# Layer norm statistics of a diffusion layer: from diagonals and full products to turned lines picked by one-pass products

## The chip, the core and the metric

The kernel runs on one core of one Trainium2 chip. The metric is the device time of one execution in microseconds; the figure for a kernel is the median of its runs. A core has TensorE (PE in the profile; its weight loads are PEld), VectorE (DVE), ScalarE (ACT), GpSimd (POOL) and SyncE (SP, here the queue of most transfers). They run side by side, each through its own list of instructions in order, and wait for each other by semaphores.

## The reference, cut to what matters

One layer over 1024 latent tokens of 1024 channels: modulation, two attention branches, a merge, a residual with layer norm, a convolutional feed-forward block, and a second residual with layer norm. The change is in the two layer norms alone:

```python
def _layer_norm(x, g, b):
    xf = x.astype(jnp.float32)
    mu = jnp.mean(xf, axis=-1, keepdims=True)
    var = jnp.mean(jnp.square(xf - mu), axis=-1, keepdims=True)
    return ((xf - mu) * lax.rsqrt(var + LN_EPS) * g + b).astype(x.dtype)
...
        x = _layer_norm(DEEPNORM_ALPHA * x + gate1 * y, ln1_g[l], ln1_b[l])

        h = x * (1.0 + scale2) + shift2
        y = _conv_ffn(h, w_up[l], conv_w[l], conv_b[l], w_down[l])
        x = _layer_norm(DEEPNORM_ALPHA * x + gate2 * y, ln2_g[l], ln2_b[l])
```

## The kernel before, in words

**Layout.** Activations lie with channels on the 128 partitions and tokens along the free dimension: eight channel tiles (KT = 8) of 128 x 1024. A mean over channels is therefore a sum over partitions and over eight tiles, and a statistic of a token has to reach all 128 partitions before it can be applied.

**Products.** A full-precision product is three one-pass products (`mm3`, L375 to L378): each operand is split by `split` (L366 to L373) into a high part (float32r) and a low part (the float32 rest, also float32r), and high x high, high x low and low x high are summed. A product of two plain float32 operands is issued as one instruction and shows as two records.

**The layer norm in pieces.** The first norm (after the product with w_out, tile y) is done in three pieces of tokens: a0 (512 tokens), a1 (256) and a2 (256). The second norm (after the down product) is done in b0 (512) and b1 (256) by the same function, `ln_steps` (L1498); its last 256 tokens go another way (`finish`, L2086), with the tokens on the partitions, and are not touched. While the channel tiles are produced, `ln_add` (L1469) sums each tile into zs and its squares into zq (ScalarE squares, VectorE or GpSimd adds, L1478 and L1479). With n = 4 or 2 tiles of 128 tokens in a piece, `ln_steps` then returns a list of steps:

- stats: 2n small products with a column of ones (L1511, L1512) give n sums and n sums of squares per token, in the PSUM tile st (128 tokens on the partitions). VectorE makes mean, square and variance (L1513, L1515, L1516), GpSimd raises to the power -1/2 (L1518), VectorE multiplies mean by it (L1519). The result is rs and mr, n columns each, tokens on partitions.
- diags: VectorE multiplies the identity by each column (L1458), which gives a diagonal of 128 x 128 per token tile, dgr for rs and dgm for mr.
- cast: two float32 products of a 128 x 128 matrix of ones with the diagonals (L1528) put each statistic on all 128 partitions (bcr, bcm in PSUM); ScalarE copies them out (L1530).
- eight applications, one per channel tile: multiply by the first (VectorE, L1535), subtract the second (VectorE or GpSimd, L1537), then the piece's outputs (for the first norm ScalarE's affine maps, L1558, and the low part, L1564).

**What sets the order.** TensorE's instructions run in the order in which the code issues them (L1390, a manual schedule for TensorE to the end). The steps of a norm are put between the products of the next work by a clock of issued columns: `tick` (L1484) adds the width of a group of three products divided by 0.8, so 640 for 512 columns and 320 for 256, and issues the next step of the list once its gap is reached, keeping what is left over. The gaps are constants, in the order first, diags, cast, first application, each further one:

```python
LN1_F = 4500.0, 5100.0, 100.0
LN1_D = (2500.0, 2000.0, 2000.0, 2500.0), (300.0, 3700.0, 300.0, 500.0), (100.0, 1000.0, 300.0, 500.0)
LN2_D = 4000.0, 2800.0, 2000.0, 1200.0, 1300.0
LN2_E = 3500.0, 1500.0, 1500.0, 500.0, 400.0
```

a0's steps fall among the y products of the second half (`y_pair`, L1650). a1's sums come at the end of the last y products, its other steps among the first products of the up projection (tile u, `up_mm`, L1759). a2's first three steps are put between a1's applications (L1677 to L1684): sums after a1's second application, diags after its fourth, cast after its eighth. b0's fall among the down products (tile p, `product`, L1951), b1's among the products of the last 256 tokens (tile yt, from L2104). VectorE, ScalarE and GpSimd are ordered by the framework's scheduler in this part, and in its order an instruction waits for those ahead of it on its engine.

**Small tiles and neighbours.** In the first norm the small PSUM tiles (st, bcr, bcm) share two banks (`sml`, L1332). The temporaries (`tm`, L1325: zs, zq, squares, diagonals) share four slots. Two weight tiles of the up projection (L1796 to L1798) are issued so that their work on VectorE comes behind a1's last diagonal (`issue_after`).

## Time and profile before

| what | value |
|---|---|
| median of 3 runs | 1521.83 us (1521.33 to 1522.35) |
| profiled execution, its own time | 1522.45 us |
| its span | 1520.6 us |
| instructions | 21967 |
| granted TensorE clock, mean | 0.998 |
| norm pieces a0, a1, a2: sums start | 816.1, 859.1, 866.3 us |
| norm pieces b0, b1: sums start | 1454.5, 1497.3 us |

The profile is of one execution. Times in it count from the start of the span. In an order of time each line gives the start, the duration, the engine, the line of the code, the operation, the tile written and the tiles read, and the shape; "x2" merges two neighbours, and a bracket tells how long the engine had been idle and who released it. Matmuls are pipelined, and the duration of one holds its way through the array: the distance from one start to the next is what it costs, not the duration.

### The profile page before, as it was taken

How to read it: one execution, taken by the hardware profiler on the slowest of the kernel's cores; microseconds unless marked ns; L12 is line 12 of the kernel's file. 1: busy time of each engine (PE TensorE's matmuls, PEld its weight loads, DVE VectorE, ACT ScalarE, POOL GpSimd, SP SyncE). 2: the span in 40 equal slices, each digit the busy share in tenths (PEclk: the TensorE clock that was granted, in tenths of full speed). 3: DMA queues.
4: the chain of work that ended last, by engine and by line, in shares of the span. 5: the costliest groups of instructions: out<-in, count | busy, mean ns of one | idle time of the engine just before them, and what ended most of it. 6: DMA issues, size and time to landing. Idle time of an engine off the chain costs nothing.

```text
span 1520.6 us, 21967 instructions
## 1 busy us (share of the span) xinstructions
PE 1507.5 (99%) x7640; PEld 1267.1 (83%) x7640; DVE 1154.0 (76%) x1735; ACT 800.3 (53%) x1406; POOL 784.7 (52%) x743
## 2 busy tenths in 40 slices
PE   9999999999999999999999999999999999999997
PEld 7888888889988888888888998888888888888886
DVE  7588847629777777787675888988888888657897
ACT  6422223448987777788233564444444444435533
POOL 0375303428896666585533556666677774021053
PEclk9999999999999999999999999999999999999999
DMA  9767673312447654823460322333344446996723
GB/s 376 257 220 256 219 242 110 94 40 66 119 119 170 170 122 105 175 66 105 154 166 22 108 90 101 111 112 111 111 111 111 111 111 192 368 270 207 253 80 111
DMA packets 112161, 229.73 MB, mean 151 GB/s; under 512 B 13521, under 2 KB 27345, under 8 KB 111954
## 3 DMA queue, kind: packets, MB, share of 16 engines
q1 hardware_dynamic: 97040, 199.72, 40.0%
q0 software_dynamic: 10400, 20.19, 8.6%
q10 hardware_dynamic: 4610, 8.42, 1.5%
q8 instruction: 60, 0.98, 0.3%
q14 instruction: 51, 0.42, 0.1%
HBM read 177.09 MB, written 65.87 MB: 160 GB/s over the span
## 4 chain that ended last, share of the span: by engine, by line
PE 44%; DVE 4%; issue 1%; DMA 1%; ACT 1%; POOL 0%; DVEq 0%; SPq 0%; ACTq 0%
PE p L377 3%; PE p L378 3%; PE p L376 3%; PE c L376 2%; PE a L376 2%; PE d L376 2%; PE a L378 2%; PE d L378 2%; PE c L378 2%; PE d L377 2%; PE c L377 2%; PE a L377 2%; PE y L378 2%; PE y L376 2%; PE y L377 2%; PE u L376 1%
## 5 line engine op out<-in xcount | busy, mean ns | idle before, releaser
L1234 DVE TENSOR_TENSOR lo<-pt,hi 128x512 fp32r<-128x512 f32 x188 | 126.8, 686 | 44.4 <-ACT hi L1228 35.0
L373 DVE TENSOR_TENSOR ld<-rd,hd 128x1024 fp32r<-128x1024 f32 x77 | 97.6, 1284 | 49.1 <-ACT hd L368 47.0
L1228 ACT CAST hi<-pt 128x512 fp32r<-128x512 f32 x188 | 108.4, 582 | 41.8 <-PE pt L847 23.5
L368 ACT CAST hd<-rd 128x1024 fp32r<-128x1024 f32 x77 | 79.5, 1050 | 86.5 <-PE p L378 53.0
L856 PE MATMUL av<-hi,VT 128*128 128x512 f32 x236 | 104.3, 443 | 0.2 <-POOL hi L1223 0.2
L377 PE MATMUL p<-ld,hd 128*128 128x512 f32 x264 | 102.8, 389 | 0.5 <-DVE ld L373 0.5
L376 PE MATMUL p<-hd 128*128 128x512 f32 x264 | 103.2, 391 | 0.0
L378 PE MATMUL p<-hd,ld 128*128 128x512 f32 x264 | 102.8, 389 | 0.0
L376 PE MATMUL g<-hh,whg 128*128 128x512 f32 x256 | 99.9, 390 | 0.0
L377 PE MATMUL g<-hl,whg 128*128 128x512 f32 x256 | 99.6, 389 | 0.0
L378 PE MATMUL g<-hh,wlg 128*128 128x512 f32 x256 | 99.6, 389 | 0.0
L856 PE MATMUL av<-lo,VT 128*128 128x512 f32 x236 | 99.3, 422 | 0.1
L373 POOL TENSOR_TENSOR wlg<-wg,whg 128x512 fp32r<-128x512 f32 x32 | 45.1, 1415 | 101.1 <-ACT whg L368 89.4
L793 DVE TENSOR_SCALAR_CACHE_REDUCE p<-s,cvt,nmc 128x1024 f32<-128x1024 f32 x64 | 85.6, 1339 | 11.0 <-PE s L760 7.1
L847 PEld LDWEIGHTS pt<-ident,p 128*128 128x128 f32 x512 | 63.6, 140 | 17.6 <-ACT rb L829 0.4
L802 ACT ACTIVATE p<-p,nm 128x1024 f32<-128x1024 f32 x64 | 73.9, 1155 | 7.0 <-DVE p L793 6.5
L847 PE MATMUL pt<-ident,p 128*128 128x128 f32 x512 | 76.6, 272 | 0.1
L759 PE MATMUL s<-KL,q 128*128 128x512 f32 (+2 forms) x186 | 72.9, 392 | 0.0
L793 DVE TENSOR_SCALAR_CACHE_REDUCE pa<-s,negsink 128x640 f32<-128x640 f32 (+1 forms) x58 | 49.3, 853 | 29.2 <-PE s L760 28.7
L368 ACT CAST wS<-s 128x512 fp32r<-128x512 f32 x76 | 45.3, 621 | 48.5 <-POOL s L1564 47.7
L760 PE MATMUL s<-KL,q 128*128 128x512 f32 (+2 forms) x186 | 69.5, 374 | 0.0
L368 ACT CAST wA<-ru 128x512 fp32r<-128x512 f32 x57 | 35.5, 623 | 63.0 <-PE d L378 34.8
(438 smaller groups left out, 5044.0 us busy)
## 6 DMA issues: line engine op xcount, KB each, us to landing
wml<-in_wmodT_dram SPq DMA_DIRECT2D x48, 512.0 KB
ru<-in_w_up_dram SPq DMA_DIRECT2D x38, 512.0 KB
rd<-td SPq DMA_DIRECT2D x55, 256.0 KB
rd<-sd SPq DMA_DIRECT2D x44, 256.0 KB
rd<-in_w_dn_dram SPq DMA_DIRECT2D x33, 256.0 KB
wm<-in_wmodT_dram SPq DMA_DIRECT2D x16, 512.0 KB
wg<-in_w_g_dram SPq DMA_DIRECT2D x32, 256.0 KB
q<-q SPq DMA_DIRECT2D x64, 128.0 KB
```

The lines of the kernel that those rows point to most:

```text
L368: cast[:] = [nc.scalar.copy(hi, src).ins]
L373: low[:] = [lo_eng.tensor_tensor(out=lo, in0=src, in1=hi.bitcast(F32), op=ALU.subtract).ins]
L376: nc.tensor.matmul(ps, a[0], b[0], start=start, stop=False, skip_group_check=resumed)
L377: nc.tensor.matmul(ps, a[0], b[1], start=False, stop=False, skip_group_check=resumed)
L378: return nc.tensor.matmul(ps, a[1], b[0], start=False, stop=stop, skip_group_check=resumed).ins
L759: nc.tensor.matmul(o, self.q1[:, hs], ks, start=True, stop=False)
L793: nc.vector.tensor_scalar(out=p if self.br else p[:, self.pad + 1:SINK + 1], in0=self.sv[h], scalar1=self.scale()[:, hs] if self.br else - ...
L802: nc.scalar.activation(o, i, AF.Exp, bias=self.nm[:, hs], scale=-1.0, accum_out=acc)
L847: nc.tensor.transpose(tr[:, h * P:(h + 1) * P], src, ident)
L856: nc.tensor.matmul(self.av, v, self.parts[n][low], start=first, stop=self.left == 0)
L1228: nc.scalar.copy(hi, units[u].parts[n])
L1234: e.tensor_tensor(out=lo, in0=src, in1=hi.bitcast(F32), op=ALU.subtract)
```

## The change

The split of the statistics now follows in stats: rs and mr lie side by side in one tile (rm, 2n columns), and VectorE splits them into a high and a low part in a tile sp of 4n columns. A new step, rows, takes the place of diags at the same gap: TensorE transposes sp (operand identr) into the unused right half of the piece's PSUM tile st, which gives 4n lines of 128 tokens, and VectorE copies them to SBUF. In cast, each statistic of each token tile is one product: the stationary operand is a column of a constant, pick, spread over 128 columns; it has ones in the high and the low line of that statistic, so 128 columns of the lines come out, summed, on all partitions. That makes 2n float32r products of 128 columns in place of two float32 products of n x 128. ScalarE's copies stay. The weights that were issued behind a1's last diagonal now come behind a1's row copy. The gaps are unchanged.

```diff
+    pick = {n: ctile([P, 2 * n], R32, f"pick{n}") for n in (2, 4)}
...
-    def diag(cols, n, nm):
-        dg = tm(f"dg{nm}", w=HALF).rearrange("p (a b) -> p a b", b=P)
-        i = nc.vector.tensor_tensor(out=dg[:, 0:n], in0=ident.unsqueeze(1).to_broadcast([P, n, P]),
-                                    in1=cols.unsqueeze(2).to_broadcast([P, n, P]), op=ALU.mult)
-        last_diag[:] = [i.ins]
-        return dg[:, 0:n].rearrange("p a b -> p (a b)")
+    for n in (2, 4):
+        nc.vector.tensor_tensor(out=pick[n], in0=ident[:, 0:2 * n], in1=ident[:, 2 * n:4 * n], op=ALU.add)
...
-            sv.extend(tiny(f"{a}{nm}") for a in ("mv", "m2", "rs", "mr"))
-            mv, m2, rs, mr = sv
+            mv, m2, rm = (tiny(f"{a}{nm}") for a in ("mv", "m2", "rm"))
+            rs, mr = rm[:, 0:n], rm[:, n:2 * n]
...
-        def diags():
-            bcs.extend(diag(c[:, 0:n], n, f"{a}{nm}") for a, c in zip("rm", sv[2:]))
-            diag_ins[nm] = last_diag[0]
+            sp = post.tile([P, 16], R32, tag="sp", name=f"sp{nm}", bufs=2)
+            split(rm[:, 0:2 * n], sp[:, 0:2 * n], sp[:, 2 * n:4 * n], nc.vector, nc.vector)
+            sv.extend((sp, st))
+
+        def rows():
+            sp, st = sv
+            turned = st[0:4 * n, P:2 * P].bitcast(R32)
+            nc.tensor.transpose(turned, sp[:, 0:4 * n], identr)
+            row = tm(f"row{nm}", R32, w=P)[0:4 * n]
+            row_ins[nm] = nc.vector.tensor_copy(row, turned).ins
+            sv[:] = [row]
 
         def cast():
             for i, a in enumerate("rm"):
                 ps = sml(f"bc{a}{nm}")[:, 0:w]
-                nc.tensor.matmul(ps, onesf, bcs[i], start=True, stop=True)
+                for t in range(n):
+                    w1 = pick[n][0:4 * n, i * n + t:i * n + t + 1].to_broadcast([4 * n, P])
+                    nc.tensor.matmul(ps[:, t * P:(t + 1) * P], w1, sv[0], start=True, stop=True)
                 o = post.tile([P, HALF], F32, tag="mrs", name=f"{a}b{nm}", bufs=2)[:, 0:w]
                 nc.scalar.copy(o, ps)
-                bcs[i] = o
+                bcs.append(o)
...
-        return [(first, stats), (gap, diags), (gap1, cast)] + [
+        return [(first, stats), (gap, rows), (gap1, cast)] + [
...
-                with tc.issue_after(diag_ins["a1"]):
+                with tc.issue_after(row_ins["a1"]):
```

More of the change, by code (lines that the diff above doesn't have):

```diff
@@ L1452, in tiny @@
         return post.tile([P, 8], F32, tag="tiny", name=name, bufs=6)
-    last_diag, diag_ins = [], {}
-    def diag(cols, n, nm):
-        dg = tm(f"dg{nm}", w=HALF).rearrange("p (a b) -> p a b", b=P)
-        i = nc.vector.tensor_tensor(out=dg[:, 0:n], in0=ident.unsqueeze(1).to_broadcast([P, n, P]),
-                                    in1=cols.unsqueeze(2).to_broadcast([P, n, P]), op=ALU.mult)
-        last_diag[:] = [i.ins]
-        return dg[:, 0:n].rearrange("p a b -> p (a b)")
+    for n in (2, 4):
+        nc.vector.tensor_tensor(out=pick[n], in0=ident[:, 0:2 * n], in1=ident[:, 2 * n:4 * n], op=ALU.add)
+    row_ins = {}
     sqs = []
```

## The prediction, made before the changed kernel ran

> **What bounds the kernel now.** I read the page first, then TensorE's waits, then the order of time around each of the five norm pieces. The page gives the span and the busy shares:

> ```profile
> span 1520.6 us, 21967 instructions
> PE 1507.5 (99%) x7640; PEld 1267.1 (83%) x7640; DVE 1154.0 (76%) x1735; ACT 800.3 (53%) x1406; POOL 784.7 (52%) x743
> PEclk9999999999999999999999999999999999999999
> ```

> TensorE is busy in 99% of the span, at full granted clock in every slice. The table of waits, TensorE's own, is complete in five lines:

> ```profile
> PE cb L522 <- DVE mhalf L404: 1.1, 1, 1.1
> PE q1acc L378 <- DVE hl L516: 0.5, 1, 0.5
> PE p L377 <- DVE ld L373: 0.5, 1, 0.5
> PE zt L2060 <- DVE zz L1923: 0.3, 1, 0.3
> PE av L856 <- POOL hi L1223: 0.2, 1, 0.2
> ```

> That is 2.6 us of waiting in 1520.6. TensorE's order is written by hand, so whatever is removed from its queue is gained and whatever it waits for is lost, nearly one for one, until about 1511 us; after that only VectorE, ScalarE, GpSimd and the stores run. So the change has two terms: products that get cheaper, and one new instruction per piece, the turning of the split statistics (rows), that TensorE must not start before VectorE is done. Before, the step at that place (diags) was VectorE work alone, and TensorE met the chain only one step later, at cast. The pieces are a0, a1, a2 (first norm, 512, 256, 256 tokens) and b0, b1 (second norm, 512 and 256).

> **The products: removed and added.** The order of time at a0's cast, and at a1's:

> ```profile
> 822.71 1.02 PE L1528 MATMUL bcra<-dgra,onesf 128*128 128x512 f32 x2
> 824.66 0.40 PE L377 MATMUL y<-ml,hwo 128*128 128x512 f32 x1
> 824.89 0.40 PE L378 MATMUL y<-mh,lwo 128*128 128x512 f32 x1
> 864.78 0.59 PE L1528 MATMUL bcra<-dgra,onesf 128*128 128x256 f32 x2
> 865.87 0.40 PE L377 MATMUL u<-B,hwu 128*128 128x512 f32 x1
> ```

> Starts of ordinary 512-wide products are 0.23 us apart (824.66 to 824.89), and one such product (L376, its row left out) stands between cast and L377. So cast holds TensorE for 824.66 - 0.23 - 822.71 = 1.72 us at a0 and 0.86 at a1. b0, also 512 wide, is put at a0's price, a2 at a1's.

> Each new product has a stationary operand of its own (one picked column, spread over 128 columns) and moves 128 columns. The nearest rows, a0's sums, where each record also loads a new 128-column operand, and the only one-pass products of 128 columns here:

> ```profile
> 816.10 0.28 PE L1511 MATMUL sta<-onec,zs 128*128 128x1 f32 x2
> 817.58 0.36 PE L1512 MATMUL sta<-onec,zq 128*128 128x1 f32 x2
> 320.68 0.23 PE L782 MATMUL s<-maskr,identr 128*128 128x128 f32 x1
> 320.74 0.33 PE L759 MATMUL s<-KC,q 128*128 128x256 f32 x1
> 336.72 0.08 PEld L824 LDWEIGHTS pts<-ident,sm 128*4 128x4 f32 x1
> 336.82 0.27 PE L824 MATMUL pts<-ident,sm 128*4 128x128 f32 x1
> 336.93 0.60 PE L847 MATMUL pt<-ident,pa 128*128 128x128 f32 x4
> ```

> Fourteen records start in the 1.48 us from 816.10 to 817.58, 0.11 us each although they move one column: the load sets the pace. A lone product of 128 columns is followed after 0.06. I take 0.11, as every new product brings a new load, and keep 0.06 as the other end. A turn of a narrow operand takes 0.11 (336.82 to 336.93). So rows and cast together cost 8 x 0.11 + 0.11 = 0.99 us for four token tiles and 4 x 0.11 + 0.11 = 0.55 for two. Gains: 0.73 each at a0 and b0, 0.31 each at a1 and a2: 2.1 us in all (3.3 at 0.06). b1 gains nothing, since VectorE is behind at the end:

> ```profile
> 1510.44 0.39 PE L378 MATMUL yt<-hd,ld 128*128 128x512 f32 x1
> 1511.62 0.68 DVE L2090 TENSOR_TENSOR ut<-yt,grow 128x512 f32<-128x512 f32 x1
> ```

> The last product ends at 1510.83 and ut starts only at 1511.62, since VectorE is still applying b1; 0.3 us less on TensorE vanishes there. [...]

> On VectorE two diagonals (0.68 us each at 512) give way to two tiny operations and a copy of a few lines; in the middle of the kernel that engine is hidden under TensorE, so I cost it at nothing. The two pick tiles are two tiny operations, nothing too. The low halves of the next weights now queue on VectorE behind the row copy in place of a1's last diagonal; both come at about 863.5 us, and their product is far off: nothing, and if a late row copy pushed them by 1 us, still nothing.

> **The new wait.** Where does rows stand in TensorE's queue? The steps are released by a count of issued products (640 for three products of 512 columns). Gap 2500 after a0's sums: after three groups. Gap 300 for a1: after one. a2 is spliced into a1's applications: after two. b0 after four, b1 after two. As a check, the same count puts a0's cast seven groups behind its sums; 817.94 to 822.71 is 4.8 us, seven times 0.68. The slot, the last statistics step on VectorE (mr, L1519), and the pace of dependent tiny operations there:

> ```profile
> 817.97 0.17 DVE L1513 TENSOR_SCALAR mva<-sta 128x8 f32<-128x8 f32 x1 [2.67 <-PE sta L1512]
> 818.17 0.17 DVE L1515 TENSOR_TENSOR m2a<-mva 128x4 f32<-128x4 f32 x1
> 819.75 0.16 DVE L1519 TENSOR_TENSOR mra<-mva,rsa 128x4 f32<-128x4 f32 x1 [1.21 <-POOL rsa L1518]
> 819.98 0.39 PE L376 MATMUL y<-mh,hwo 128*128 128x512 f32 x1
> 860.66 0.40 PE L376 MATMUL u<-B,hwu 128*128 128x512 f32 x1
> 862.01 0.16 DVE L1519 TENSOR_TENSOR mra<-mva,rsa 128x2 f32<-128x2 f32 x1 [0.59 <-POOL rsa L1518]
> 862.09 0.42 DVE L1478 TENSOR_TENSOR zs<-zs,z 128x256 f32<-128x256 f32 x1
> 862.43 0.42 DVE L1458 TENSOR_TENSOR dgra<-ident,rsa 128x256 f32<-128x256 f32 x1
> 868.62 0.40 PE L376 MATMUL u<-B,hwu 128*128 128x512 f32 x1
> 870.47 0.69 DVE L1519 TENSOR_TENSOR mra<-mva,rsa 128x2 f32<-128x2 f32 x1 [1.29 <-POOL rsa L1518]
> 871.08 0.41 DVE L1458 TENSOR_TENSOR dgra<-ident,rsa 128x256 f32<-128x256 f32 x1
> 871.10 0.99 POOL L1564 TENSOR_TENSOR B<-v,B 128x256 fp32r<-128x256 f32 x1
> 871.41 0.96 DVE L1458 TENSOR_TENSOR dgma<-ident,mra 128x256 f32<-128x256 f32 x1
> 1458.56 0.16 DVE L1519 TENSOR_TENSOR mrb<-mvb,rsb 128x4 f32<-128x4 f32 x1 [1.15 <-POOL rsb L1518]
> 1459.09 0.39 PE L376 MATMUL p<-hd 128*128 128x512 f32 x1
> 1499.68 0.16 DVE L1519 TENSOR_TENSOR mrb<-mvb,rsb 128x2 f32<-128x2 f32 x1 [0.83 <-POOL rsb L1518]
> 1499.82 0.39 PE L376 MATMUL yt<-hd 128*128 128x512 f32 x1
> ```

> After mr come the two halves of the split, each 0.20 us after its predecessor (817.97 to 818.17), the second 0.16 long; then 0.03 for the release (the sums end at 817.58 + 0.36 = 817.94, VectorE starts at 817.97) and 0.10 from load to product (336.72 to 336.82). So the turn can start 0.20 + 0.20 + 0.16 + 0.03 + 0.10 = 0.69 us after mr starts. Against the slot:
> a0: 819.75 + 0.69 - 819.98 = 0.46. b0: 1458.56 + 0.69 - 1459.09 = 0.16. b1: 1499.68 + 0.69 - 1499.82 = 0.55.
> a1: 862.70 - 860.66 = 2.04 if nothing comes between; an accumulation (L1478) took the place right after mr and cost 0.34, so I take 2.4; with one more, 2.8.
> a2: hi where dgra was, 871.08, lo 0.20 later, turn at 871.08 + 0.49 = 871.57: 2.95. But the diagonal in lo's place took 0.96 where its twin took 0.41, beside GpSimd's L1564: 0.55 more, 3.5. Lo is a subtraction of two SBUF operands like that diagonal, so I take 3.5. [...]

> Sum of waits 0.46 + 2.4 + 3.5 + 0.16 + 0.55 = 7.1 us. Behind the waiting turn stand the ordinary products (y, u, p, yt), then cast and all the rest, in one queue; nothing later has slack to give it back, as the waits table showed. b1's wait delays yt, from which VectorE's last chain starts, so it counts in full, with b1's turn, 0.11.

> **Sum.** -2.1 + 7.1 + 0.1 = +5.1 us. The profiled execution took 1522.45 us (span 1520.6 and 1.85 around it), so 1527.5; the median of the three runs, 1521.83, is 0.6 below it, so I forecast 1526.9. Ends of the forecast itself: a1 at 2.04 and a2 at 2.95, each of the five waits one step of 0.20 shorter, and the gain of 3.3 give 5.2 + 0.1 - 3.3 = +2.0; a1 at 2.8, a2 another 0.34 later, each wait 0.20 longer, and the gain of 2.1 give 8.9 + 0.1 - 2.1 = +6.9. So 1523.8 to 1528.7.

> **Rivals.**
> No wait (faster): VectorE's chain is done when TensorE reaches rows, because the order around it moves or TensorE is later there. Decides from waits under 2 us. -2.0 to -3.2 with b1's turn paid, 1518.6 to 1519.8. For it: b0 lacks only 0.16; against it: GpSimd's power alone ends after the slots of a1 and a2. 0.07.
> Half the wait: split and power get ahead of the accumulations, the loads hide as in the 0.06 row; +0.5 to +2.0, 1522.3 to 1523.8. 0.18.
> The clock falls in a2's wait. The rows by stretch show one lowered clock:

> ```profile
> 1511.00:1520.00 9.00, 0.00 (x0) 0.00 (x0) 5.73 (x12) 3.06 (x6) 3.21 (x4) 0.77 0.44 147
> ```

> A mean of 0.77 over 9 us without a product is, if the clock halves, 4.1 us at half, starting 4.9 us after the stretch begins. 3.5 is less than that. If it fell, 4.1 us at half would cost 2 us more: 1528.9. [...] 0.07.
> Not one pass: if a 128-column product of this kind were paid like the full ones, four passes, cast keeps its 1.72 and 0.86 and only the turns and waits remain: 7.1 + 5 x 0.11 = +7.7 us, 1529.5. Against it: the 0.06 row. 0.05.
> The forecast keeps 0.63.

> **Numbers.** 0.2% is 3 us, about what a measurement of this kernel can tell from no change. Faster takes about half of the first rival and a rest: 0.05. Same takes the other half, nearly all of the second, and a little of the forecast below +3: 0.21. Slower: 0.74. The range 1523.0 to 1529.0 leaves out the first rival, a third of the second, and the last.

> **What would show it.** In the profile after: TensorE's waits list rows' turn on VectorE five times, about 7 us, most at a1 and a2; starts of the new products 0.11 apart; cast shorter by 0.8 us at 512; the clock full. Wrong if the turn's waits at a1 or a2 are under 1 us, or if the low part of the split comes much later than 0.4 us after mr.

## The result, and the profile after

The changed kernel takes 1544.92 us (median of 4 runs, 1543.78 to 1545.80), the kernel before 1521.58 us (4 runs, 1521.05 to 1522.35). The ratio is 1.0154, 95% interval 1.0141 to 1.0167: 23.3 us slower, where 5.1 were forecast. The profiled execution took 1543.78 us, 21.3 more than that of before. Further down, one run each of e11, of e12 and of the kernel before came out far longer (2155, 1665 and 3074 us), and the ratios leave them out.

The page of the changed kernel, its span, busy shares and granted clock:

```profile
span 1542.0 us, 21995 instructions
PE 1523.4 (99%) x7653; PEld 1268.5 (82%) x7653; DVE 1153.6 (75%) x1742; ACT 799.9 (52%) x1406; POOL 791.5 (51%) x743
PEclk9999999999999999999999999999999999999999
```

TensorE has 13 records more and is busy for 15.9 us longer (1523.4 against 1507.5). So most of the loss is not waiting, and this alone says that the forecast's sum, which was made of waits, cannot hold all of it. TensorE's waits in the changed kernel (total, times, longest):

```profile
PE sta L1523 <- DVE spa L373: 6.2, 3, 3.7
...
PE stb L1523 <- DVE spb L373: 0.3, 1, 0.3
```

These are the turns that were forecast, 6.5 us of idle time. The table counts from the modelled end of the product ahead; counted from the slot, as in the prediction, each is some 0.16 longer. The order of time at a0, a1 and a2:

```profile
821.00 0.39 PE L378 MATMUL y<-mh,lwo 128*128 128x512 f32 x1
821.63 0.23 PE L1523 MATMUL sta<-identr,spa 128*16 128x128 f32 x1 [0.24 <-DVE spa L373]
...
861.68 0.39 PE L378 MATMUL u<-B,lwu 128*128 128x512 f32 x1
864.28 0.22 PE L1523 MATMUL sta<-identr,spa 128*8 128x128 f32 x1 [2.22 <-DVE spa L373]
...
872.07 0.40 PE L378 MATMUL u<-B,lwu 128*128 128x512 f32 x1
876.21 0.22 PE L1523 MATMUL sta<-identr,spa 128*8 128x128 f32 x1 [3.74 <-DVE spa L373]
...
876.87 0.63 PE L378 MATMUL u<-B,lwu 128*128 128x512 f32 x1
877.29 0.63 PE L376 MATMUL u<-B,hwu 128*128 128x512 f32 x1
```

From the start of the product ahead, less its 0.23: 0.40, 2.37 and 3.91 us late. Soon behind a2's turn the products start 0.42 apart (876.87 to 877.29) instead of 0.23. The rows by stretch (length, TensorE busy and records, granted clock, DMA share, GB/s) say why:

```profile
874.00:878.00 4.00, 1.79 (x6) 0.84 0.28 98
878.00:881.00 3.00, 3.00 (x10) 0.65 0.25 87
```

If the clock halves, 0.84 over 4 us is 1.3 us at half and 0.65 over 3 us is 2.1: together 3.4 us, from 0.5 us behind the wait on (876.71 to 880.13 in the trace's clock records). The page's digits don't show it, since one digit stands for 38 us.

The two waits and the clock are over by 881 us, but most of the loss comes later. The same view, TensorE alone, over two stretches in which it does nothing but 512-wide products, first before, then after:

```profile
1000.00:1100.00 100.00, 100.00 (x443) 1.00 0.35 118
1300.00:1400.00 100.00, 100.00 (x443) 1.00 0.91 276
```

```profile
1000.00:1100.00 100.00, 100.00 (x434) 1.00 0.31 106
1300.00:1400.00 100.00, 100.00 (x431) 1.00 0.97 294
```

TensorE is busy without a gap, at full clock, in both kernels, and does 9 and 12 products fewer in 100 us. The stretches hold only products that the change doesn't touch (up and down projections). By the starts in the two traces, neighbouring 512-wide products stand 0.2267 us apart before, and after 0.231 on average in the up projection and 0.233 in the down projection. The same product runs 8.8 us later than before at 897 us, and 20.4 us later at 1412 us.

**Where the 21.3 us are,** by matching the starts of the same products in both traces: 0.5 within the first 20 us of the span; 12.7 from slower 512-wide products (11.6 of them between 897 and 1412 us; the 1.1 between 750 and 897 are partly what the other terms leave over); 7.1 in the waits of the turns; 1.5 from the halved clock; -0.4 from the casts, turns included.

### The profile page after: what moved, and what is told of

Same layout as the page of the kernel before. It is cut to its first block, busy times and chain, and to the rows that moved or that the text cites. A ratio compares the mean times of both kernels' runs of the same rounds, so it can differ in the third digit from the quotient of the medians.

```text
span 1542.0 us, 21995 instructions
## 1 busy us (share of the span) xinstructions
PE 1523.4 (99%) x7653; PEld 1268.5 (82%) x7653; DVE 1153.6 (75%) x1742; ACT 799.9 (52%) x1406; POOL 791.5 (51%) x743
## 4 chain that ended last, share of the span: by engine, by line
PE 95%; DVE 3%; POOL 1%; issue 1%; DMA 0%; ACT 0%; DVEq 0%; POOLq 0%; ACTq 0%
PE av L857 7%; PE pt L848 6%; PE g L376 4%; PE g L378 4%; PE g L377 4%; PE p L376 4%; PE p L377 4%; PE p L378 4%; PE s L760 3%; PE s L761 3%; PE d L376 2%; PE a L378 2%; PE d L378 2%; PE c L377 2%; PE c L376 2%; PE d L377 2%
## 5 line engine op out<-in xcount | busy, mean ns | idle before, releaser
L373 DVE TENSOR_TENSOR ld<-rd,hd 128x1024 fp32r<-128x1024 f32 x77 | 98.8, 1299 | 52.1 <-ACT hd L368 50.0
L376 PE MATMUL p<-hd 128*128 128x512 f32 x264 | 105.1, 398 | 0.0
L377 PE MATMUL p<-ld,hd 128*128 128x512 f32 x264 | 104.3, 395 | 0.0
L378 PE MATMUL p<-hd,ld 128*128 128x512 f32 x264 | 104.0, 394 | 0.0
L376 PE MATMUL g<-hh,whg 128*128 128x512 f32 x256 | 99.9, 390 | 0.0
L378 PE MATMUL g<-hh,wlg 128*128 128x512 f32 x256 | 99.7, 389 | 0.0
L377 PE MATMUL g<-hl,whg 128*128 128x512 f32 x256 | 99.7, 389 | 0.0
L373 POOL TENSOR_TENSOR wlg<-wg,whg 128x512 fp32r<-128x512 f32 x32 | 45.5, 1427 | 101.8 <-ACT whg L368 89.9
```

The costliest lines, as they stand in the source:

```text
L373: low[:] = [lo_eng.tensor_tensor(out=lo, in0=src, in1=hi.bitcast(F32), op=ALU.subtract).ins]
L376: nc.tensor.matmul(ps, a[0], b[0], start=start, stop=False, skip_group_check=resumed)
L377: nc.tensor.matmul(ps, a[0], b[1], start=False, stop=False, skip_group_check=resumed)
L378: return nc.tensor.matmul(ps, a[1], b[0], start=False, stop=stop, skip_group_check=resumed).ins
```

## The experiments

**The theories.** What made untouched products slower? The change adds two small constants, pick for 2 and for 4 tiles. The memory planner puts constants and some tiles at the lower end of SBUF, one behind the other, and others at the upper end. The two constants take 64 bytes of every partition, and every tile behind them at the lower end moves by 64 bytes, while the upper end stays. In the planner's addresses one tile of T13h, an operand of the up projection, moves from byte 89312 to 89376, and one of its weights, wS, stays at 151520; both had the remainder 224 by 256, and now the first has 32. Theory **placement**: the products slow down because the two groups of operands no longer stand at the same remainder. Rival **turn**: the later, sparser order behind the waits, or the new products, slow the rest of the kernel. Then, of the first 7 us: are they the waits, and what does the clock cost? The kernel before is measured afresh in each round of runs.

### Placement in the kernel before, and half a period more in the changed one

e2 is the kernel before with a constant that nobody reads (each such tile is also filled once by GpSimd, left out below). e1 is the changed kernel with the same, e3 the changed kernel with 64 bytes at the upper end instead.

```diff
...
+    padt = ctile([P, 16], F32, "padt")      # e1, e2
...
+    rp = tc.alloc_tile_pool(name="rp", bufs=1, side="right", reuse_waits="tile")   # e3
+    padr = rp.tile([P, 16], F32, tag="padr", name="padr")
...
```

> The kernel before, with a constant of 64 bytes per partition that nothing uses (one GpSimd fill at the start) and nothing else changed. Theory A: about 12 us slower, 1533 to 1535 us, with 512-wide starts 0.231 to 0.236 us apart from about 750 us on, as in the changed kernel. Theory B: 1521.6 us, no change.

> The changed kernel with one more constant of 64 bytes per partition beside pick, so that the tiles allocated from the lower end of SBUF lie 128 bytes, not 64, above their places in the kernel before. Theory A (placement: the two pick tiles take 32 bytes each, everything above them on that side moves by 64 bytes, the tiles allocated from the upper end do not, and products whose operands or neighbours differ by 64 modulo 128 start about 5 ns further apart): the drift of about 12 us from 890 us on goes, 512-wide starts are 0.227 us apart again, and about 1531 us is left, the waits of the turns and a stretch of halved clock. Theory B (the slower products come from the changed steps themselves: re-phased engines, or the clock): nothing moves, about 1544 us.

> The changed kernel with a 64-byte tile at the upper end of SBUF, so that the tiles allocated from there move by 64 bytes too: all operands of the 512-wide products then lie at 32 modulo 128, in place of 96 before and a mixture in the changed kernel. Theory A in the form that it is the mixture that costs: about 1531 us, starts 0.227 us apart. Theory A in the form that 96 is a good place and 32 a bad one: all products slow, 1544 us or more. Theory B: 1544 us.

e2 took 1535.48 us, ratio 1.0089 [1.0074, 1.0104], 13.7 us slower than before (1521.83). Its stretches:

```profile
1000.00:1100.00 100.00, 100.00 (x434) 1.00 0.33 110
1300.00:1400.00 100.00, 100.00 (x430) 1.00 0.93 285
```

Its norms are those of the kernel before, none of its turns exists, and the pace is that of the changed kernel. The rival turn is out for this part: placement alone costs 13.7 us.

e1 took 1541.74 us, 1.0133 [1.0118, 1.0149], and e3 1542.35, 1.0138 [1.0121, 1.0155]. In both, the distance of the two groups has become 128 bytes, from different sides, and the products are hardly quicker (434 and 435 in the second stretch, for 431). e1's stretch:

```profile
1300.00:1400.00 100.00, 100.00 (x434) 1.00 0.97 295
```

(Part of what they gain is lost again to the clock: its mean over the profiled execution is 0.996 in both, 0.997 in the changed kernel.) So a period of 128 bytes, my first idea, falls, and the expected 1531 us with it, and that both kernels agree says that it is the distance that counts and not where either end stands.

### A whole period more

e5 is the changed kernel with 192 bytes more at the lower end, 256 with the two constants; e6 has the 192 bytes at the upper end.

```diff
+    padt = ctile([P, 48], F32, "padt")      # e5
...
+    padr = rp.tile([P, 48], F32, tag="padr", name="padr")      # e6
```

> The changed kernel with 192 more bytes of constants, so that the tiles allocated from the lower end lie 256 bytes above their places in the kernel before. In the kernel before, all operands of the 512-wide products from 760 us on lie at 224 modulo 256; e1 to e3 mixed two remainders and were all slow. Theory A2 (it is a mixture of remainders modulo 256 that costs): all at 224 again, starts 0.227 us apart, no drift from 890 to 1410 us, and the waits and the halved clock alone remain, 1529 to 1531 us. Rival (any move away from the places of the kernel before costs, or a longer period): 1540 to 1545 us as e1.

> The changed kernel with a 192-byte tile at the upper end: all operands from 760 us on at 32 modulo 256, none where it was in the kernel before. Theory A2: as e5, 1529 to 1531 us. Rival (224 is a good remainder, 32 a bad one, or only the old places are fast): 1540 us or more.

e5 took 1533.62 us, 1.0077 [1.0062, 1.0092], and e6 1532.62, 1.0067 [1.0052, 1.0082]. e5's stretches:

```profile
1000.00:1100.00 100.00, 100.00 (x442) 1.00 0.31 106
1300.00:1400.00 100.00, 100.00 (x443) 1.00 0.95 295
```

The pace of the kernel before is back, with the constants, the turns and the new products in place: 11.3 us of the 23.3 are gone (1544.92 to 1533.62, across two rounds in which the kernel before differs by 0.1), although the clock, as below, costs 2.7 us more here. That is part of why e5 and e6 miss the 1529 to 1531 us that were expected. What is left are the waits and the clock. e5's waits:

```profile
PE sta L1525 <- DVE spa L373: 6.2, 3, 3.7
```

and its stretches at the end of a1's wait (the turn starts at 863.60) and behind it:

```profile
863.00:866.00 3.00, 2.40 (x7) 0.50 0.00 0
866.00:869.00 3.00, 3.00 (x9) 0.50 0.77 254
```

Here the clock halved already within a1's wait of 2.2 us (0.95 from 859 to 863 us, so from about 862.6 on), for 6.8 us (0.66 from 860 to 870), and again for 3.4 us behind a2's (0.96 from 876 to 880, 0.62 from 880 to 884). In the starts this costs 4.2 us (2.7 and 1.5), against 1.5 in the changed kernel.

### Two controls: 32 bytes, and 256 bytes, in the kernel before

```diff
+    padt = ctile([P, 8], F32, "padt")       # e11
+    padt = ctile([P, 64], F32, "padt")      # e12
```

> The kernel before, with a constant of 32 bytes: tiles from the lower end at 0 modulo 256, those from the upper end at 224 as before, a difference of 32. Theory A2 (any mixture of remainders modulo 256): slow as e2, 1533 to 1536 us. Rival (32 bytes is too little to matter, only larger distances do): 1521 to 1524 us.

> The kernel before, with an unused constant of 256 bytes more at the lower end of SBUF, so that every tile allocated from that end lies 256 bytes further and again has the remainder by 256 of the tiles at the upper end; nothing else. Theory of the remainder by 256 bytes: the time of the kernel before, 1521 to 1523 us. Rival, that any extra constant or any shift costs (its clearing, the fit of the memory, or the neighbourhood of two tiles): about 1535, as with 32 and 64 bytes.

e11 took 1534.93 us, 1.0087 [1.0068, 1.0105]; e12 took 1521.63, 1.0001 [0.9991, 1.0012]. The second stretch of e11 and of e12:

```profile
1300.00:1400.00 100.00, 100.00 (x433) 1.00 0.93 287
```

```profile
1300.00:1400.00 100.00, 100.00 (x443) 1.00 0.91 274
```

An unused constant cost nothing here when it was 256 bytes long (1521.63 us), and 13 us when it was 32 (1534.93). All kernels on one line each, with the distance between the two groups of operands from the planner's addresses:

| kernel | distance, bytes | products, 1300 to 1400 us |
|---|---|---|
| before | 0 | 443 |
| e11 | 32 | 433 |
| e2, after | 64 | 430, 431 |
| e1, e3 | 128 | 434, 435 |
| e5, e6, e12 | 256 | 443 |

### The waits, taken away by other gaps

e4 and e7 give the gaps ahead of each turn more room and take as much from the gap behind it; e4 with the placement of e1, e7 with that of e5. e8 does it for a2 alone. e9 is e7 with a2's cast two groups later.

```diff
-LN1_D = (2500.0, 2000.0, 2000.0, 2500.0), (300.0, 3700.0, 300.0, 500.0), (100.0, 1000.0, 300.0, 500.0)
-LN2_D = 4000.0, 2800.0, 2000.0, 1200.0, 1300.0
-LN2_E = 3500.0, 1500.0, 1500.0, 500.0, 400.0
+LN1_D = (3100.0, 1400.0, 2000.0, 2500.0), (2900.0, 1100.0, 300.0, 500.0), (600.0, 500.0, 300.0, 500.0)
+LN2_D = 4000.0, 3400.0, 1400.0, 1200.0, 1300.0
+LN2_E = 3500.0, 2100.0, 900.0, 500.0, 400.0
...
-                for n, step in zip((a[1], a[3], a[7]), second):
+                for n, step in zip((a[0] - 1, a[5], a[7]), second):
...
+    (600.0, 1780.0, 300.0, 500.0)           # e9, the last piece of LN1_D
```

> As e1, with the gaps of the norm steps set so that each turn comes about one (a0, b0, b1) to four (a1) groups of products later while cast keeps its place, and a2's sums put before a1's first application, its turn after the sixth. My account of the change: no turn waits, no halved clock, and what is left is the cheaper casts, 1519 to 1520.5 us, faster than both kernels. Rival (the turns and the small products cost more on TensorE than I count, or the chain is late wherever it stands): 1523 us or more.

> e4's timing of the norm steps (no turn waits) with e5's placement. My account: placement back and waits gone leave only the cheaper casts, 1519 to 1520.5 us, faster than the kernel before. Rival (the waits were not the local loss, or the placement still costs): 1523 us or more.

> e5's placement, and of the new timing only a2's: its sums ahead of a1's first application, its turn after the sixth. The wait at a2 (3.7 us) goes and with it, if the clock fell because of that wait, the stretch at half clock (1.7 us); the waits at a0, a1 and b1 stay (3.3 us). With the clock's share 5.4 us below e5, without it 3.7 us below.

> As e7, with a2's cast two groups of products (1.4 us) later: in e7 the copy of a2's lines stood on VectorE behind applications and TensorE waited 1.4 us for it at the cast. If that wait is what keeps e7 from the gain of the cheaper casts, 1.4 us below e7 and below the kernel before by 1 us or more (1520 to 1521 us); if the scatter of e7 (1522 to 1528) has another source, the profile shows no wait but the median stays at 1523 us.

e4 took 1533.45 us, 1.0076 [1.0061, 1.0091]: 8.3 less than e1, and what is left is about the price of e1's placement (434 products in the stretch, as in e1). e7 took 1523.81, 1.0014 [1.0005, 1.0024]: 9.8 less than e5. Both miss the 1519 to 1520.5 us that were expected. In e7's waits no turn stands any more, but a new line does:

```profile
PE bcra L1535 <- DVE rowa L1527: 1.4, 1, 1.4
```

a2's row copy now stands on VectorE behind applications of a1, and the cast waits for it. e8, with 1529.39 us and 1.005 [1.0035, 1.0065], is 4.2 below e5; its waits:

```profile
PE sta L1525 <- DVE spa L373: 2.9, 3, 2.2
```

Of the three turns only a2's has gone, 3.3 us of idle time, and with it the halved clock behind a2 (1.00 from 874 to 881 us) but not the one at a1 (0.52 from 863 to 866 us, 0.50 from 866 to 869). The expectation set 3.7 against 5.4, without and with a share of the clock; 4.2 lies between and does not decide it.

e9 took 1522.55 us, 1.0011 [1.0003, 1.002]. No turn or cast of the first norm waits for the chain, the clock is full where it fell in the others (1.00 from 859 to 869, 874 to 881 and 1459 to 1465 us; mean 0.998, as before), and still the time is 1.1 above that of the kernel before (1521.48), where 1520 to 1521 was expected. So a change with its waits, its clock and its placement put right breaks even: the casts bring nothing that a measurement of this kernel can tell. None of these kernels beats the kernel before.

### The clock: the same waits, filled with products

e10 is e5 with products that nobody reads, put ahead of the turns of a1 (16) and a2 (28), so that TensorE works where it waited.

```diff
+            for _ in range({"a1": 16, "a2": 28}.get(nm, 0)):
+                nc.tensor.matmul(st[:, 2 * P:4 * P], identr, tp["B", 0, 0][:, 0, 0:2 * P], start=True, stop=True)
```

> As e5, with products that nothing reads put into TensorE's queue ahead of the turns of a1 (16) and a2 (28), 256 columns wide, 0.12 us each by the profile before: 1.9 and 3.4 us of work in place of most of the waits of 2.2 and 3.7 us. If the halved clock of e5 (6.8 us after a1, 3.4 us after a2) follows from the idle time, it goes, and the time falls by about 4 us, to 1529 to 1530 us, although the turns come no earlier. If the waits alone are the local loss, nothing changes, 1533.5 us.

e10 took 1530.6 us, 1.0057 [1.0043, 1.007], 3.0 below e5 for an expected 4. The turns still come when the chain is done; TensorE's idle time there is 1.0 us in place of 6.2:

```profile
PE sta L1527 <- DVE spa L373: 1.0, 3, 0.4
...
PE stb L1510 <- DVE zq L1477: 0.3, 1, 0.3
```

and the rows by stretch, at a1 and at b0:

```profile
863.00:866.00 3.00, 3.00 (x15) 1.00 0.48 128
866.00:869.00 3.00, 3.00 (x20) 1.00 0.58 227
...
1462.00:1465.00 3.00, 3.00 (x8) 0.50 0.87 292
```

At a1 the clock is full where e5 has 0.50, and it is full behind a2 too (1.00 from 874 to 884 us). For a2 that shows the idle time of the wait as the cause, since the clock fell in the changed kernel, e5 and e6, which have the full wait of 3.7 us there (0.65, 0.78 and 0.58 from 878 to 881 us). For a1 it fits, but with the same wait of 2.2 us the clock fell in e5, e6 and e8 (0.50, 0.57 and 0.52 from 863 to 866 us) and stayed full in the changed one. And in the same execution it halved at b0 (0.96 from 1459 to 1462 us, so from about 1461.8 on, and 0.50 from 1462 to 1465), with only b0's sums, 2 us of products of one column, and the wait of 0.3 us among them (second line) ahead of it. The products then start 0.42 apart in place of 0.23, which took back about 1.5 us up to 1465, and in the profiled executions e10 is 4.7 below e5.

The clock records in the traces of the changed kernel and of the one before give the times more exactly. In the changed kernel the clock is full from 13.141 to 876.713 us, half for 3.413 us, and full again from 880.126 to 1535.485; in the kernel before it is full from 10.561 to 1515.839. The full parts are 253, 192 and 441 times 3.4133 us long, so within each of the two executions all these times stand on one grid of that step. In the changed kernel a line of the grid (876.713 less four steps) lies at 863.06, in the middle of a1's wait: of its sums and wait 2.0 us fall into the step before, 1.2 into the one behind, and the clock stays. Counted in the same way, the 3.41 us ahead of a fall hold 2.9 us at a2 in the changed kernel, 2.2 at a1 in e5 (a1's sums, 0.8, and the first 1.4 of the wait), 1.9 at a2 in e5 (by 0.78 from 878 to 881 us the fall comes at 879.7, and the turn started at 878.2), and 2.1 at b0 in e10 (the sums and the wait among them, 1458.60 to 1460.73). My reading, an estimate from these five: one-column products weigh much like waiting, and whether the wait of 2.2 us lowers the clock depends on where in it a line of the grid lies. A threshold they don't show: 1.9 us lowered the clock once, and 2.0 did not once. What places the grid, the runs don't show either.

## Why the prediction was wrong, step by step

**The waits of the turns: right in sum, by other steps at a1 and a2.** Forecast 0.46, 2.4, 3.5, 0.16 and 0.55, sum 7.1. Measured from the slots 0.40, 2.37, 3.91, none, and 0.46 (0.3 in the table of waits and 0.16 for the modelled end): 7.1. At a1 two accumulations, not one, came between mr and the turn, each at less than was added for one. VectorE at a2 in the changed kernel:

```profile
874.13 0.67 DVE L1515 TENSOR_TENSOR rma<-mva,rma 128x2 f32<-128x2 f32 x1 [1.28 <-POOL rma L1514]
...
875.07 0.69 DVE L372 CAST spa<-rma 128x4 fp32r<-128x4 f32 x1
875.67 0.41 DVE L1542 TENSOR_TENSOR z<-z,mba 128x256 f32<-128x256 f32 x1
876.00 0.15 DVE L373 TENSOR_TENSOR spa<-rma,spa 128x4 fp32r<-128x4 f32 x1
```

The forecast had the low part (L373) lengthened beside GpSimd. It took 0.15 us; what made it late was the high part (L372), 0.69 beside GpSimd's L1569 (874.75 to 875.73) for 0.16 at a1, and an application of a1 that took the place between the two. The low part started 1.87 us after mr, where the prediction had named "much later than 0.4 us" as a sign of being wrong; that the sum still agrees is partly luck. The 0.55 that the forecast added for the low part came from one diagonal that ran beside GpSimd's L1564; the low part ran with no GpSimd operation beside it. mr took 0.67 beside GpSimd's L1542 (874.07 to 874.79), for 0.16 at a1 with none beside it. The forecast's upper end also has two small slips: one more accumulation at a1 makes 2.72, not 2.8, and its waits add up to 8.8, not 8.9.

**"The two pick tiles are two tiny operations, nothing too": this step failed.** Their two operations take 0.16 us each on VectorE at 777.0 us and no wait follows from them, but their 64 bytes moved every tile behind them at the lower end, and that cost 12.7 us in the profiled execution; alone, in e2, 13.7. No wait and no instruction of the change shows it. The prediction's list of what would show it wrong has no line for it either: it looked at the new instructions only, and took the duration of all others as given.

**The cheaper casts: the size was off.** Forecast -2.1 with the turns. The order of time of the changed kernel at a0's cast and at a1's:

```profile
824.33 0.40 PE L378 MATMUL y<-mh,lwo 128*128 128x512 f32 x1
824.65 0.66 PE L1533 MATMUL bcra<-rowa,pick 16*128 16x128 f32 x4
825.15 0.60 PE L1533 MATMUL bcma<-rowa,pick 16*128 16x128 f32 x4
825.69 0.50 PE L376 MATMUL y<-mh,hwo 128*128 128x512 f32 x1
826.02 0.40 PE L377 MATMUL y<-ml,hwo 128*128 128x512 f32 x1
...
868.31 0.40 PE L378 MATMUL u<-B,lwu 128*128 128x512 f32 x1
868.64 0.43 PE L1533 MATMUL bcra<-rowa,pick 8*128 8x128 f32 x2
868.91 0.38 PE L1533 MATMUL bcma<-rowa,pick 8*128 8x128 f32 x2
869.22 0.50 PE L376 MATMUL u<-B,hwu 128*128 128x512 f32 x1
869.56 0.40 PE L377 MATMUL u<-B,hwu 128*128 128x512 f32 x1
```

Four new products take 0.50 us (824.65 to 825.15), 0.125 each for the 0.11 forecast; the change from a wide product to them and back adds 0.09 and 0.10 (824.33 to 824.65, and 825.69 to 826.02, less 0.23), which wasn't in the sum. So a0's cast costs 826.02 - 0.23 - 824.56 = 1.23 us, and a1's 869.56 - 0.23 - 868.54 = 0.79, for 1.72 and 0.86 before. With turns of 0.14 (821.63 to 822.00, less 0.23) the gain is 0.35 at a0 and b0 each, and a loss of 0.07 at a1 and a2 each: 0.6 in place of 2.1, and less than 0.5 with b1's turn. The rival with four passes is out: a quarter of a full float32 product's 0.86 us (822.71 to 823.57 before) would be 0.215 for 128 columns, and the new ones took 0.125.

**The falling clock: a rival came true.** It had 0.07 and a price of 2 us; it cost 1.5 in the profile of the changed kernel, behind a2's wait as the rival had put it, and up to 4.2 in e5. The prediction had read from one row that 4.9 us without a product go ahead of a fall. In the runs less was enough: of the 3.41 us ahead of the fall behind a2 in the changed kernel 2.9 were idle (873.30 to 876.21), and in e5 and e10 falls came behind 1.9 to 2.2 us of waiting and one-column sums. So "3.5 is less than that" was no protection, and that the clock held at a1 in the changed kernel, where the same wait lowered it in e5, e6 and e8, was luck.

**The sum.** For the profiled execution the forecast was 1527.5. It lacks 12.7 of placement, 1.5 of the clock, 1.6 of the casts and 0.5 at the start: 16.3, and 1527.5 + 16.3 = 1543.8. The medians stand 2.0 further apart than the two profiled executions do (after's lies 1.1 above its profile, before's 0.9 below; the forecast took 0.6 below).

## What to carry to other kernels

A constant or a small tile is not free because its operations are: it moves what the planner puts behind it, and in e2 64 unused bytes cost 13.7 us. Where TensorE is busy throughout, compare the number of equal products in 100 us of an untouched stretch, before and after, ahead of any story about the change itself (443 and 431 here); if they differ, pad the new tiles to a multiple of 256 bytes per partition, which brought the 443 back in e5 and kept them in e12, and measure the change alone. And a step that gets shorter on TensorE by moving its work into a chain on another engine has to be given a later slot, or the wait eats the gain: here 7.1 us of waits for 0.6 us.

## What the runs showed of the hardware that was not expected

```profile
520.00:700.00 180.00, 180.00 (x1072) 1.00 0.50 110
```

In the changed kernel the records are as many, 1072.

In e5 the clock halved for a wait that is clearly shorter than the stretch that it then stayed low: 2.2 us of waiting, 6.8 us at half. The same wait lowered it in e6 and e8 too and not in the changed kernel, where a line of the 3.4133 us grid cuts the wait in two, as told at e10. So a wait of 2 us or more had a second price in these runs, between nothing (a1 in the changed kernel) and 2.7 us (a1 in e5). e9's runs, without such waits, still spread from 1521.61 to 1525.60 us; what sets the higher ones stays open.
